# Hybrid Hyena and neighbourhood-attention step: activations and three weight blocks of a row block loaded in one transfer, with the order of the opening changed

## The chip, the cores and the metric

The kernel runs on one core of a Trainium2 chip. The metric is the device time of one execution in microseconds (us); a kernel's time is the median of its runs. Before the change it is 869.93 us, the median of three runs (867.72 to 872.84).

The engines are named as the profile names them: PE (TensorE, matrix products), PEld (its weight loads), DVE (VectorE), ACT (ScalarE), POOL (GpSimd) and SP (SyncE, which here only issues transfers).

## The reference

One layer of a network is applied to 128 context tokens and 512 latent tokens. Both groups share the weights. What matters here is the beginning: a modulation (scale, shift and gate) is computed from a condition, the tokens are scaled and shifted by it, and the result is projected by a wide matrix. The first three of the projected parts go through a short convolution; the filters of the long convolution come from a small network on a fixed embedding.

```python
shift, scale, gate = modulation(cond, p["w_ada"], p["b_ada"])   # silu(cond) @ w_ada + b_ada
h = x * (1 + scale) + shift
z = h @ w_in                       # (640, 1024) @ (1024, 10240), split into hy, g_h, qkv, g_a, m
hy = short_conv(hy, conv_w, conv_b)
hf = sin(f_freq[0] * (z_emb @ f_w1 + f_b1))      # the filter network, on a fixed embedding z_emb
hf = sin(f_freq[1] * (hf @ f_w2 + f_b2))
hf = (hf @ f_w3) * decay
...
x_new = layer_norm(ALPHA * x + gate * out, p["ln_g"], p["ln_b"])
```

## The kernel before, in words

The 640 tokens stand as columns; the 1024 channels are eight **row blocks** of 128. `hH` and `hL` hold the modulated tokens `h`, split into a high part (rounded to the type fp32r) and the rest, of the same type. The wide matrix is cut into column blocks of 128 columns, each a 128 x 1024 array in `a["wall"]`, eight 128 x 128 tiles side by side (one for each row block). A weight block is split in the same way, into `wh` and `wl`. A product of a row block with a column block is three passes, `wh` with `hH`, `wl` with `hH`, `wh` with `hL` (line 170, `accumulate`), each of two matmuls of 320 tokens: six matmuls, summed over the eight row blocks in two PSUM banks.

**The prologue** (lines 258 to 388) makes `h` one row block k at a time, and multiplies it at once with three column blocks, 0, 8 and 1, whose sums stay open over all eight k (`mm` for blocks 0 and 8, `mm1lo` and `mm1hi` for block 1). For each k it does this:

- Two transfers of 512 KB bring row block k's two parts of the modulation matrix (`ada`, line 247); PE multiplies them with the condition (`adaT`, line 253, 32 matmuls), ACT copies the result (`row`, line 328), and PE turns it (`modT`, line 357). DVE adds the bias (`mod`, line 362).
- A transfer brings the tokens of row block k (`xt`, from `xT`, 320 KB). DVE computes `hx` (line 369), ACT computes `hH` from the same operands (line 370, two instructions), and DVE takes the difference `hL` (line 378).
- The tiles of weight blocks 0, 8 and 1 come in four steps, not in eight: `SPAN` on line 277 gives columns 0 to 128 with k = 0, 128 to 256 with k = 1, 256 to 512 with k = 2 and 512 to 1024 with k = 3, so twelve transfers (`raw`, `w1r`). ACT makes the high parts (line 300), DVE and, for blocks 8 and 1 from k = 2 on, POOL the low parts (line 304).
- The table `script` says which products PE does at which of four places of an iteration: "00" is block 0 with row block 0, "81" is block 8 with row block 1, "w5" is five matmuls on a zeroed tile (line 270) that keep PE busy and whose result is not used.
- The filter network (`sin_layer`, from line 214, its products `ps_f` on line 221, its sines on line 234) advances by some steps in each iteration, as the table `layers` says.

Inside the prologue the order on PE, DVE and ACT is that of the code. SP issues its transfers in an order of its own queue; a transfer into a buffer that is still read waits, and everything behind it on SP waits too. `ada` has three buffers, `raw` three. The scheduler orders what stands behind the prologue.

Behind the prologue PE multiplies column block 9 (its split is the tile `w9`), then block 2, then 10, with the first filter spectrum between them. From block 2 on the low part of a weight block is not computed by DVE: ACT writes the negative of the raw block rounded (line 149), and a transfer issued by POOL adds the weights themselves onto it (line 150). The filter spectrum needs constants: a Fourier matrix (`draw`, from `dft`, split into `dftH` and `dftL`), a second small one (`gs`), the filter weights (`w3s`, `w3h`, `w3l`) and the convolution's weights (`pack2`).

## Time and profile before

| what | value |
|---|---|
| median of three runs | 869.93 us (867.72 to 872.84) |
| the profiled execution's own time | 871.15 us |
| its span, first to last instruction | 869.3 us |
| so outside the span | 1.85 us |
| PE busy | 856.0 us, 98% |
| DVE, ACT, POOL busy | 678.7, 465.5, 137.8 us |
| bytes moved | 139.17 MB, mean 160 GB/s |
| granted PE clock, mean of the span | 0.995 |

A row of the timeline gives the start in us from the span's start, the duration, the engine, the line, the operation, the output and input tiles with their shapes and, after x, how many instructions are merged in it; square brackets give the engine's idle time before it and what ended it. A row of the windows view gives for a stretch of time its length, then the busy time of PE, PEld, DVE, ACT and POOL (with counts), the granted PE clock as a share of full speed, the busy share of the transfer engines and the bytes per second that they moved.

### The profile page before, as it was taken

The numbers are of one execution on the slowest core, as the hardware profiler recorded it, in microseconds if no ns is written. First come the engines' busy times: TensorE is split into PE (matmuls) and PEld (weight loads), VectorE is DVE, ScalarE is ACT, GpSimd is POOL, SyncE is SP. The second block draws the span as 40 slices with busy tenths as digits, with TensorE's granted clock in tenths as the row PEclk, the third lists the DMA queues.
The fourth block names the chain that finished last, engine by engine and source line by source line (L and its number), as shares of the span: only waits on it lengthen the run. The fifth ranks groups of instructions, "written<-read, shape, count | busy, mean of one in ns | idle before, by whom it ended". The sixth has DMA issues, their size and how long they took to land.

```text
span 869.3 us, 16872 instructions
## 1 busy us (share of the span) xinstructions
PE 856.0 (98%) x6394; PEld 827.1 (95%) x6394; DVE 678.7 (78%) x1407; ACT 465.5 (54%) x1001; POOL 137.8 (16%) x146
## 2 busy tenths in 40 slices
PE   8899999999999999999999999999999999999996
PEld 7799999999999999999999999999999999999885
DVE  5476678669567865999987898889888769799776
ACT  4385554654645454547566566556666655345300
POOL 0210101010100101105222224024322200000000
PEclk9999999999999999999999999999999999999998
DMA  9987757456665647874343526263454376445621
GB/s 313 369 212 174 149 106 155 112 149 136 137 152 118 144 114 186 209 202 163 116 162 111 185 76 221 73 207 101 149 155 133 104 260 212 165 132 147 245 99 49
DMA packets 58740, 139.17 MB, mean 160 GB/s; under 512 B 8703, under 2 KB 25219, under 8 KB 58660
## 3 DMA queue, kind: packets, MB, share of 16 engines
q1 hardware_dynamic: 47140, 111.69, 39.0%
q0 software_dynamic: 5904, 20.71, 14.9%
q10 hardware_dynamic: 5616, 5.70, 1.9%
q8 instruction: 50, 0.82, 0.4%
q14 instruction: 30, 0.25, 0.1%
HBM read 121.96 MB, written 16.12 MB: 159 GB/s over the span
## 4 chain that ended last, share of the span: by engine, by line
PE 96%; DMA 3%; DVE 1%; ACT 0%; POOL 0%; issue 0%; DVEq 0%; POOLq 0%
PE sp L1195 33%; PE mm L170 31%; PE out L1548 6%; PE v L926 5%; PE pt L1028 3%; PE s L1035 3%; PE s L988 2%; PE mm L184 2%; DMA ada<-wada 2%; PE ve L938 1%; DMA wl<-wall 1%; PE adaT L253 1%; PE adaT L270 1%; PE yb L159 1%; PE yb L158 1%; PE yb L160 1%
## 5 line engine op out<-in xcount | busy, mean ns | idle before, releaser
L1195 PE MATMUL sp<-t,wb 128*128 128x320 f32 x912 | 142.0, 310 | 0.0
L1195 PEld LDWEIGHTS sp<-t,wb 128*128 128x128 f32 x912 | 135.2, 188 | 0.9 <-ACT pp L1056 0.5
L170 PE MATMUL mm<-hH,wh 128*128 128x320 f32 x480 | 113.3, 313 | 0.3 <-ACT hH L370 0.3
L170 PE MATMUL mm<-hL,wh 128*128 128x320 f32 x480 | 113.1, 311 | 0.0
L170 PE MATMUL mm<-hH,wl 128*128 128x320 f32 x480 | 112.9, 311 | 0.1
L1195 PE MATMUL sp<-hH,wb 128*128 128x320 f32 x456 | 111.2, 314 | 0.0
L170 PEld LDWEIGHTS mm<-hH,wh 128*128 128x128 f32 x480 | 80.2, 189 | 2.4 <-issue 1.2
L170 PEld LDWEIGHTS mm<-hH,wl 128*128 128x128 f32 x480 | 81.1, 189 | 1.1 <-DMA wl<-wall 0.5
L170 PEld LDWEIGHTS mm<-hL,wh 128*128 128x128 f32 x480 | 81.0, 189 | 0.9 <-DVE hL L378 0.4
L101 ACT ACTIVATE wb<-s 128x512 fp32r<-128x512 f32 x92 | 56.5, 629 | 45.9 <-DVE s L1155 26.7
L150 POOL DMA_DIRECT2D wl<-wall x38 | 33.1, 871 | 300.9 <-ACT wl L149 224.3
L1195 PEld LDWEIGHTS sp<-hH,wb 128*128 128x128 f32 x456 | 78.5, 188 | 2.3 <-issue 2.1
L151 ACT ACTIVATE wh<-raw 128x1024 fp32r<-128x1024 f32 x38 | 40.4, 1062 | 73.5 <-PE mm L170 65.4
L1195 PE MATMUL sp<-hL,wb 128*128 128x320 f32 x228 | 70.4, 309 | 0.0
L102 DVE TENSOR_TENSOR wb<-s,wb 128x512 fp32r<-128x512 f32 x92 | 62.5, 691 | 8.0 <-ACT wb L101 8.0
L101 ACT ACTIVATE wb<-raw 128x512 fp32r<-128x512 f32 x66 | 41.5, 628 | 47.3 <-PE sp L1195 23.4
L1010 POOL TENSOR_SCALAR p<-p,sm 128x384 f32<-128x384 f32 x32 | 44.6, 1406 | 101.7 <-DVE sm L1009 101.7
L102 DVE TENSOR_TENSOR wb<-raw,wb 128x512 fp32r<-128x512 f32 x66 | 46.5, 704 | 5.1 <-ACT wb L101 4.8
L170 PE MATMUL mm<-yhs,wh 128*128 128x320 f32 x256 | 47.9, 309 | 0.0
L1210 DVE TENSOR_TENSOR c<-sp,u 128x320 f32<-128x320 f32 x69 | 33.5, 486 | 12.1 <-PE sp L1195 12.1
L1195 PEld LDWEIGHTS sp<-hL,wb 128*128 128x128 f32 x228 | 42.9, 188 | 0.0
L1010 POOL TENSOR_SCALAR edge<-edge,sm 128x320 f32<-128x320 f32 x32 | 42.2, 1330 | 0.5 <-DVE sm L1009 0.5
(384 smaller groups left out, 2054.0 us busy)
## 6 DMA issues: line engine op xcount, KB each, us to landing
raw<-wall SPq DMA_DIRECT2D x93, 512.0 KB, 3.6
wl<-wall POOLq DMA_DIRECT2D x38, 512.0 KB, 5.8
ada<-wada SPq DMA_DIRECT2D x16, 512.0 KB, 7.0
tm<-bias SPq DMA_DIRECT2D x16, 512.0 KB, 4.9
gate<-wgate SPq DMA_DIRECT2D x8, 512.0 KB, 4.0
wo<-wall SPq DMA_DIRECT2D x8, 512.0 KB, 5.4
xt<-xT SPq DMA_DIRECT2D x8, 320.0 KB, 7.6
dec<-decay SPq DMA_DIRECT2D x20, 128.0 KB, 3.3
```

The source lines that it names most:

```text
L101: hi = nc.scalar.activation(dst_h, src, AF.Copy)
L102: return hi, (eng or nc.vector).tensor_tensor(dst_l, src, f(dst_h), op=ALU.subtract)
L150: nc.gpsimd.dma_start(wl, a["wall"][i], accum_op=ALU.add)
L151: nc.scalar.activation(wh, raw[:], AF.Copy)
L170: nc.tensor.matmul(ps[hf][:, :HALF], wt[k], x[:, hf * HALF : (hf + 1) * HALF], start=(i == 0 and k == 0), stop=(i == lead[2] and k == NK - ...
L926: nc.tensor.matmul(ps[t // 2][:, t % 2 * 256 : t % 2 * 256 + 256], x[:, k, P * t : P * t + P], wk, start=first and t % 2 == 0, stop=last, ...
L1010: nc.gpsimd.tensor_scalar_mul(pv, pv, sm[:, 2:3])
L1028: nc.tensor.transpose(pt[:, i * P : i * P + P], x, ident)
L1035: nc.tensor.matmul(dst, lhs, rhs, start=start, stop=stop, skip_group_check=True)
L1195: nc.tensor.matmul(dst, wk, x(xi, k), start=j < 4 and k == 0 and i == 0, stop=k == 3 and i == 2, skip_group_check=True,)
L1210: after = nc.vector.tensor_tensor(c, dst, c if j == 3 else u, op=ALU.add)
L1548: ins = nc.tensor.matmul(dst, m[k][:, c0 : c0 + P], w[:, c : c + n], start=(first and k == 0), stop=(last and k == 5), skip_group_check=True,)
```

## The change

The host lays out a new array `xw`: for each row block k the 640 tokens and, beside them, the three 128 x 128 tiles of weight blocks 0, 8 and 1 that belong to k. One transfer of 512 KB for each k brings both. `SPAN`, its twelve transfers and the functions around it are gone. ACT makes the three high parts of k in one instruction (`wf`, 128 x 384) and DVE the three low parts in one (`wg`); POOL has none of it. The tiles `xw` take the three buffers of `raw`.

The embedding and the first filter constants (`zemb`, 82.5 KB, and `pack1`, 98 KB) are loaded ahead of the modulation matrix, and the first filter layer starts among PE's opening matmuls. The product "00" moves from k = 0 to k = 1. `gs`, `skip`, `pack2` and the Fourier matrix are loaded behind the last row block, and the split of the Fourier matrix and of `gs` stands behind the prologue (`dft_high`, `dft_consts`, with `behind` setting who follows whom). Weight block 2 is split by ACT and DVE, without the adding transfer.

```diff
         script = (
-            ("w16", "w5", "w3", "w6 00"), ("", "", "80", "10"), ("", "", "01", "81 11"), ("", "", "02", "82 12"),
+            ("w8", "w3", "w8", ""), ("", "", "00", "80 10"), ("", "", "01", "81 11"), ("", "", "02", "82 12"),
...
-        layers = ((0, 4), (0, 2), (0, 1), (0, 1), (0, 1), (0, 3), (0, 3), (0, 1))
+        layers = ((0, 2), (1, 0), (1, 2), (0, 2), (0, 2), (1, 1), (0, 0), (0, 0))
...
-        SPAN = {0: (0, 128), 1: (128, 256), 2: (256, 512), 3: (512, 1024)}
...
-        def w_load(i, g):
-            load_to(span(i, g)[0], a["wall"][i][:, slice(*SPAN[g])])
...
+        out["zemb"] = temp("u", "zemb", 4)[:33]
+        load_to(out["zemb"], a["zemb"])
+        load_pack(1)
...
         for k in range(NK):
+            xw = wp.tile([P, 1024], F32, tag="raw", bufs=3, name=f"xw{k}")
             psa = aux(f"adaT{k}")
+            if k == 0:
+                work("w8", psa)
+                step(5)
...
+            load_to(xw[:], a["xw"][k])
+            xt, wf = xw[:, :NT], xw[:, NT:]
+            wh = row(yhp, "yh", f"wf{k}", F32R)[:, : 3 * P]
+            wl = row(yhp, "yh", f"wg{k}", F32R)[:, : 3 * P]
...
-            xt = row(yhp, "yh", f"xt{k}")
-            load_to(xt[:], a["xT"][:, k])
-            if k in SPAN:
-                for i in (8, 1) if k == 0 else (0, 8, 1):
-                    w_load(i, k)
...
+            if k >= 6:
+                split(wh, wl, wf)
+            if k == 7:
+                wraw(9)
                 load_pack(2)
...
+                wraw(2)
+                load_filter(0)
...
+                nc.scalar.activation(w9[:, 0], raws[9][:], AF.Copy)
...
-            if k == 3:
-                w_high(0, 3)
-            else:
-                for i in (8, 1) if k < 5 else ():
-                    w_high(i, min(k, 3))
-            if k in SPAN:
-                w_low(0, k)
+            if k < 6:
+                nc.scalar.activation(wh, wf, AF.Copy)
             nc.vector.tensor_tensor(hL[:, k], hx[:], f(hH[:, k]), op=ALU.subtract)
+            if k < 6:
+                nc.vector.tensor_tensor(wl, wf, f(wh), op=ALU.subtract)
...
-                early[2] = wtile(2, "dma")
+                early[2] = wtile(2)
...
         prologue()
-    tc.keep_in_program_order(last[0])
-    head = quarter_head(0)
-    next(head)
+        opening = list(last)
+        head = quarter_head(0)
+        next(head)
+        dft_high(0, 1)
+    tc.keep_in_program_order(opening[0])
     dft_consts()
```

How the order of the engines' instructions moves, at three places. The names are those of the program; a number behind a name is that of its buffer, and x with a count stands for equal instructions in a row.

**SP, from the program's first transfer to the second row block's.** Before:

```order
L63 DMA pack_80<-pack 128x34
L63 DMA ada_127<-wada 128x1024 x2
L63 DMA raw_169<-wall 128x128
L63 DMA xt_182<-xT 128x640
L63 DMA raw_172<-wall 128x128
L63 DMA w1r_175<-wall 128x128
L63 DMA pack_187<-pack 128x196
L63 DMA zemb<-zemb 33x640
L63 DMA ada_239<-wada 128x1024 x2
L63 DMA E<-gs 128x256
L63 DMA skip_719<-hydr 1x256
L63 DMA xt_260<-xT 128x640
```

And in the changed kernel (`pack_119` holds the first filter constants, `pack_187` above):

```order
L63 DMA pack_80<-pack 128x34
L63 DMA zemb<-zemb 33x640
L63 DMA pack_119<-pack 128x196
L63 DMA ada_157<-wada 128x1024 x2
L63 DMA xw_136<-xw 128x1024
L63 DMA ada_217<-wada 128x1024 x2
L63 DMA xw_215<-xw 128x1024
L63 DMA ada_275<-wada 128x1024 x2
L63 DMA xw_273<-xw 128x1024
```

Two small transfers now stand ahead of the first modulation matrix; behind it there are three transfers of 512 KB for each row block and nothing else.

**PE, from its first instruction to the second row block's modulation.** Before:

```order
L270 MATMUL adaT_126<-hid 128x256 x16
L253 MATMUL adaT_126<-ada_127,st 32x128 x8
L270 MATMUL adaT_126<-hid 128x256 x5
L253 MATMUL adaT_126<-ada_127,st 32x128 x8
L270 MATMUL modT_191<-hid 128x256 x3
L357 MATMUL modT_191<-pack_80,row_167 128x2 x2
L270 MATMUL modT_191<-hid 128x256 x6
L170 MATMUL mm_0_210<-hH,wh_170 128x320
```

In the changed kernel:

```order
L274 MATMUL adaT_137<-hid 128x256 x8
L225 MATMUL ps_f_147<-zemb,pack_119 64x320
L225 MATMUL ps_f_148<-zemb,pack_119 64x320
L274 MATMUL adaT_137<-hid 128x256 x8
L257 MATMUL adaT_137<-ada_157,st 32x128 x8
L274 MATMUL adaT_137<-hid 128x256 x3
L257 MATMUL adaT_137<-ada_157,st 32x128 x8
L274 MATMUL modT_192<-hid 128x256 x8
L339 MATMUL modT_192<-pack_80,row_187 128x2 x2
L257 MATMUL adaT_216<-ada_217,st 32x128 x16
L174 MATMUL mm_0_130<-hH,wf_190 128x320
L174 MATMUL mm_1_131<-hH,wf_190 128x320
```

The filter layer's products `ps_f` come among the filler matmuls, and the first product (`mm_0` from `hH`) stands behind the second row block's `adaT`, no longer ahead of it.

**ACT, from the last `hH` of the prologue to the first rounding for an adding transfer (`wl`, from `raw`).** Before:

```order
L370 ACTIVATE hH<-xt_617,mod_636 128x512
L101 ACTIVATE w_644<-raw_621 128x1024
L149 ACTIVATE wl_648<-raw_623 128x1024
L561 ACTIVATE zs_102<-mm_0_210 128x128
L563 ACTIVATE zs_102<-mm_0_210 128x8x8
L564 ACTIVATE zs_102<-mm_0_210 128x8x16
L151 ACTIVATE wh_647<-raw_623 128x1024
L234 ACTIVATE E<-E 128x640
```

In the changed kernel:

```order
L352 ACTIVATE hH<-xw_573,mod_627 128x512
L105 ACTIVATE wh_636<-raw_605 128x1024
L540 ACTIVATE zs_102<-mm_0_130 128x128
L542 ACTIVATE zs_102<-mm_0_130 128x8x8
L543 ACTIVATE zs_102<-mm_0_130 128x8x16
L544 ACTIVATE zs_102<-mm_1_131 128x8x40
L540 ACTIVATE zs_106<-mm_0_132 128x128
L542 ACTIVATE zs_106<-mm_0_132 128x8x8
L546 ACTIVATE u_670<-zs_102,pack_603 128x641
L380 ACTIVATE dftH<-draw 128x640 x2
```

The high part of block 9 (`w_644`), the rounding of block 2 (`wl_648`) and the second sine (`E` from `E`) no longer stand behind the last `hH`; the first two pieces of the Fourier matrix (`dftH`) now do.

More of the change, by code (lines that the diff above doesn't have):

```diff
@@ L259, in prologue, with warm @@
         script = (
-            ("w16", "w5", "w3", "w6 00"), ("", "", "80", "10"), ("", "", "01", "81 11"), ("", "", "02", "82 12"),
+            ("w8", "w3", "w8", ""), ("", "", "00", "80 10"), ("", "", "01", "81 11"), ("", "", "02", "82 12"),
             ("", "", "03", "83 13"), ("", "", "04", "84 14"), ("", "", "05", "85 15"), ("", "", "06", "86 16 07 87 17"),
         )
-        layers = ((0, 4), (0, 2), (0, 1), (0, 1), (0, 1), (0, 3), (0, 3), (0, 1))
+        layers = ((0, 2), (1, 0), (1, 2), (0, 2), (0, 2), (1, 1), (0, 0), (0, 0))
         nc.gpsimd.memset(f(hid[:, :256]), 0.0)
+        front = (0, 8, 1)
+        parts = {}
+        def warm(ps, n):
+            for _ in range(n):
+                nc.tensor.matmul(ps[:, 256:], hid[:, :P], hid[:, :256], start=True, stop=True, skip_group_check=True)
         def work(items, ps):
@@ L392, in prologue @@
         now(filt)
+        last.append(low)
     dftH = hyc.tile([P, 2, 5, 2, P], F32R, tag="dftH", name="dftH")
@@ L418, in dft_consts @@
         load_to(gs, two(a["gs"]))
+        behind(last[0], opening[0])
         split(gsH[:], gsL[:], gs)
@@ L442, in filter_spectrum @@
         load_to(skip[:], a["hydr"][q : q + 1])
+        if q == 0:
+            behind(last[0], opening[0])
         w3h = hwa.tile([P, 512], F32R, tag="w3h", name=f"w3h_{q}")
```

79 lines of the change are left out of this document (22 added, 57 removed).

## The prediction

> **What bounds the kernel now.** I read the page's first and fourth parts, then the windows view by stages, then the timeline of PE.
>
> ```profile
> span 869.3 us, 16872 instructions
> PE 856.0 (98%) x6394; PEld 827.1 (95%) x6394; DVE 678.7 (78%) x1407; ACT 465.5 (54%) x1001; POOL 137.8 (16%) x146
> PE 96%; DMA 3%; DVE 1%; ACT 0%; POOL 0%; issue 0%; DVEq 0%; POOLq 0%
> PE adaT L253 <- DMA ada<-wada: 2.9, 3, 1.7
> ```
>
> PE is the bound almost everywhere; the one wait of PE that the waits view finds of any size is for `ada`, at the start. So what an edit to the prologue is worth is read from the prologue alone: by how much sooner PE gets through it.
>
> ```profile
> 5.35:10.80 5.45, 4.94 (x51) 3.73 (x50) 1.18 (x5) 1.82 (x5) 0.00 (x0) 1.00 1.03 352
> 10.80:26.90 16.10, 14.87 (x169) 12.16 (x171) 13.35 (x29) 8.23 (x20) 2.00 (x2) 1.00 1.00 362
> 26.90:36.10 9.20, 7.35 (x58) 5.88 (x58) 2.88 (x7) 2.63 (x5) 2.62 (x2) 0.81 1.03 414
> 36.10:51.70 15.60, 15.57 (x180) 14.42 (x181) 11.48 (x22) 8.94 (x17) 0.81 (x1) 1.00 0.78 273
> 51.70:66.50 14.80, 14.70 (x99) 14.26 (x98) 11.43 (x16) 12.11 (x26) 1.95 (x3) 1.00 0.87 199
> ```
>
> Up to 36.1 us the transfer engines are full (1.00 and over) and PE has gaps; from 36.1 on PE is full and they are not. Between 26.9 and 36.1 the granted PE clock is 0.81. So the prologue is bound by transfers, then by a slow clock, and by PE alone only in its last third. While small pieces (rows of 512 and 1024 bytes of `raw` and `w1r`) were among the transfers they moved 352 to 362 GB/s; later, with rows of 2 KB and more, 414.
>
> ```profile
> 26.88 0.64 PE L253 MATMUL adaT<-ada,st 128*32 128x128 f32 x16 [1.07 <-DMA ada<-wada]
> 29.24 0.64 PE L253 MATMUL adaT<-ada,st 128*32 128x128 f32 x16 [1.71 <-DMA ada<-wada]
> 31.16 0.87 PE L170 MATMUL mm<-hH,wh 128*128 128x320 f32 x2
> 34.62 1.34 PE L221 MATMUL ps_f<-hf,pack 64*128 64x320 f32 x4
> 40.43 1.08 PE L253 MATMUL adaT<-ada,st 128*32 128x128 f32 x32
> 42.79 0.54 PE L170 MATMUL mm<-hH,wh 128*128 128x320 f32 x2
> 44.73 1.08 PE L253 MATMUL adaT<-ada,st 128*32 128x128 f32 x32
> 51.60 0.31 PE L170 MATMUL mm1hi<-hL,w1h 128*128 128x320 f32 x1
> ```
>
> In the full part one row block takes PE 44.73 - 40.43 = **4.30 us** (1.0 for `adaT`, 0.36 for `modT`, 18 products at 0.147, the rest gaps; 0.147 is a twelfth of the stretch from 42.79 to 44.73 less its gap of 0.18). The rows at 26.88 and 29.24 are the two waits, and the pair at 31.16 takes 0.87 where the one at 42.79 takes 0.54: the slow clock. The last matmul of the prologue starts at 51.60; block 9's first follows at 51.74.
>
> **The change, part by part.** I count to two marks: t1, when PE has done row block 1's `modT`, and t7, the same for row block 7.
>
> ```profile
> 1.18 0.89 SPq L63 DMA_DIRECT2D ada<-wada  x2
> 1.64 3.78 PE L270 MATMUL adaT<-hid 128*128 128x256 f32 x16 [1.64 <-POOL spare L312]
> 5.35 1.08 PE L253 MATMUL adaT<-ada,st 128*32 128x128 f32 x16
> 6.37 1.27 PE L270 MATMUL adaT<-hid 128*128 128x256 f32 x5
> 7.57 0.65 PE L253 MATMUL adaT<-ada,st 128*32 128x128 f32 x16
> 9.58 0.96 PE L270 MATMUL modT<-hid 128*128 128x256 f32 x6 [0.25 <-DVE mod L362]
> 12.16 1.29 PE L221 MATMUL ps_f<-zemb,pack 33*64 33x320 f32 x4
> 15.37 0.50 PE L357 MATMUL modT<-pack,row 128*128 128x2 f32 x4
> 46.73 0.50 PE L357 MATMUL modT<-pack,row 128*128 128x2 f32 x4
> ```
>
> With the next PE instruction 0.36 us behind the start of `modT`, t1 is now 15.7 and t7 47.1, 31.4 apart; five full row blocks would be 21.5 of that.
>
> *The opening.* Up to about 7.6 us a filler takes 0.24 us (3.78 / 16), at 9.58 only 0.16. The early products run at the slow pace, and for `ps_f` no row shows that: its bounds are 1.29 as at 12.16 and twice that. I take 2.1, the ratio of the pairs at 31.16 and 42.79 (0.87 / 0.54 = 1.6) times 1.29. PE then does 8 fillers, `ps_f`, 8 fillers in 3.78 + 2.1 from 1.64: 7.5. Two `adaT` halves at 0.65, three fillers 0.5, eight fillers 1.25 and `modT` 0.55 bring row block 0's `modT` to 11.1. (`ada` arrives earlier: two more issues, at 0.89 / 2 each, on SP and 180 KB ahead of it put it about 1 us behind now, when PE took its first half at 5.35 without waiting for it.)
>
> *The first products, now behind `adaT` 1.* They need the chain `modT`, `mod`, `hH`, `hL`, `wg`:
>
> ```profile
> 20.98 0.42 DVE L304 TENSOR_TENSOR wl<-raw,wh 128x256 fp32r<-128x256 f32 x1
> 25.93 0.69 DVE L304 TENSOR_TENSOR wl<-raw,wh 128x512 fp32r<-128x512 f32 x1 [0.95 <-ACT wh L300]
> 42.97 0.16 DVE L362 TENSOR_TENSOR mod<-modT,bss 128x4 f32<-128x4 f32 x1 [0.24 <-PE modT L357]
> 43.16 1.21 ACT L370 ACTIVATE hH<-xt,mod 128x128 fp32r<-128x128 f32 x2 [1.14 <-DVE mod L362]
> 44.40 0.83 DVE L378 TENSOR_TENSOR hL<-hx,hH 128x640 fp32r<-128x640 f32 x1 [0.43 <-ACT hH L370]
> 45.14 1.68 DVE L230 SCALAR_TENSOR_TENSOR E<-E 128x640 f32<-128x640 f32 x2
> 46.85 0.49 DVE L232 TENSOR_SCALAR E<-E 128x640 f32<-128x640 f32 x1
> ```
>
> No row shows `wg`, 128x384; between 0.42 and 0.69 I take 0.55. From `mod`'s start: `hH` ends at 1.40, `hL` at 2.26, `wg` at 2.8. So from 11.1 the first row block's `wg` is there at 13.9, while PE has finished `adaT` 1 at 12.1 and waits (its first pass, 0.3, fits into that). Two more passes, 0.6, and `modT` 0.35: **t1 = 14.9**, 0.8 sooner than now.
>
> *Row blocks 1 to 7.* PE needs 4.30 for each, and 1.2 more in the second, where the second filter layer's products now stand. 6 x 4.30 + 1.2 = 27.0, against 31.4: 4.4 saved, the two waits and the slow clock. What covers the rest:
> - `wg`, at `mod` + 2.8, is asked for at `mod` + 3.3 (12 products 1.77, gap 0.2, `adaT` 1.0, the first pass 0.3). Cover 0.5.
> - DVE has per row block the chain to 2.8 and at most two filter steps, 1.68 less overlaps: 4.4. That may lose 0.1 once; it takes 0.55 for `wg` in place of its own low parts now, and POOL's, of which there are none left.
> - ACT, busy for 8.94 of 15.60 us in the full part, gets `wf` (128x384) in place of the three high parts.
> - Transfers: 1.57 MB per row block, 3.8 us at 414 GB/s and 4.3 at 362. From a bulk start at about 3 us even the slower rate brings `ada` 7 (12.3 MB) to 37, some 2 us ahead of its use at t7 - 2.5. SP's queue holds three kinds of waits, for `ada`'s readers, for DVE's `wg` three row blocks before, and for an earlier transfer; each of them is answered at least two row blocks ahead.
>
> t7 = 14.9 + 27.0 = **41.9**, now 47.1.
>
> *The last products and behind.* From t7: 12 products of blocks 8 and 1 at k = 6, then 18 at k = 7, 30 x 0.147 = 4.4, and about 0.2 of waiting for `hL`, as ACT now makes `w9`'s high part (below, 1.04) ahead of the last `hH`. 46.5 in place of 51.7: **5.2 saved**. Behind it block 2 no longer waits for an adding transfer:
>
> ```profile
> 48.57 1.04 ACT L101 ACTIVATE w<-raw 128x1024 fp32r<-128x1024 f32 x1
> 60.10 0.30 PEld L170 LDWEIGHTS mm<-hH,wl 128*128 128x128 f32 x2 [0.54 <-DMA wl<-wall]
> 58.28 1.14 ACT L149 ACTIVATE wl<-raw 128x1024 fp32r<-128x1024 f32 x1
> 59.72 0.87 POOL L150 DMA_DIRECT2D wl<-wall x1 [7.80 <-ACT wl L149]
> DMA to landing us min/median/max: 5.6/7.2/9.2
> ```
>
> PE's own rows lose only 0.1 there (14.80 less 14.70), so I credit 0.1. Late next is block 10, whose `wl` starts on ACT now at 58.28. Between the last `hH` and it ACT loses `w9`, block 2's rounding, a sine and `hid`, and gains `dftH` and `gs`, about 1.8 us fewer; the last `hH` ends at t7 + 1.7. That puts it at 51.4, POOL's issue at 52.8, landing by 5.6 to 9.2 at 58.4 to 62.0. PE asks for it after blocks 9 and 2 (96 products, 14.1), two filter products (about 0.5) and four of its own (0.6): at 61.7. I take 0; its bounds are 0 and 0.3 as worked out, up to 2 when ACT is held up.
>
> *Far behind,* the scheduler put some instructions of the attention stage in another order, of the same kinds and number. No row prices that. PE's idle time after 66.5 is 7.9 us in all:
>
> ```profile
> 66.50:869.30 802.80, 794.89 (x5829) 773.11 (x5827) 637.86 (x1328) 428.78 (x926) 129.30 (x123) 1.00 0.53 149
> ```
>
> I take 0, with 1 us either way.
>
> **Sum**: -0.8 - 4.4 - 0.1 = **-5.3**. The profiled execution took 871.15 (its span of 869.3 and 1.85 around it), 1.22 over the median of the runs; it would take 865.9, and the median **864.6**.
>
> **The rivals.**
> - *The slow clock comes back.* It followed a stretch in which PE did 0.64 us of work in 3.4 (25.8 to 29.2), and cost 3.46 us for 12 products (31.16 to 34.62) that take 1.77 otherwise. In the changed opening PE idles for about 1.4 of 3.4 us ahead of the first `wg`. If that is enough, the next 12 products and `adaT` cost some 2.3 more: 866.9. Against it: the gaps are shorter and PE has done 9 us of work. [...]
> - *Block 10's low part is late.* ACT and POOL run later by up to 2 us: 866.6. For it: 9.2 is the longest landing in just this stretch. Against it: ACT has less to do.
> - *The change doesn't do what it says:* transfers bind on, at 362 GB/s, and t1 slips as `ada` 1 comes at 12.5. A rate of 362 costs nothing by the sum above, so only t1 slips, to 15.5, with 0.5 of waits later: 865.7.
> - *Slower.* The three `xw` buffers close a loop: transfer k + 3 is issued when DVE has done `wg` of k, 2.8 us behind its `mod`, and must have landed at `mod` k + 3. A round is then (2.8 + landing) / 3. At the longest landing of now, 10.3 of `ada` under full queues, that is 4.37, no matter. To eat up the 5.3 over the five rounds that reuse a buffer, each must take 5.36: landings over 13.3 us; to lose 0.5%, 4.35 us more, over 15.9. Then 870 to 875.
>
> ```profile
> DMA to landing us min/median/max: 4.5/7.0/10.3
> ```
>
> **How the numbers follow.** Forecast 0.60 (its own range 862.8 to 866.4: t1 moves by 0.8 with the bounds of `ps_f` and of the filler pace, the attention stage by 1). Clock 0.12, block 10 0.11, transfers 0.09, slower 0.08. The range for eight in ten takes in all but the slower case and the ends of the clock's and of block 10's: **862.0 to 868.4**. A difference of 0.5%, about what a measurement of this kernel can tell from no change, is 4.35 us, so faster begins at 865.6. Some three quarters of the forecast's range lie below it, and half of the transfers' case; with a little off for the spread of the runs, faster 0.55. Slower than 874.3 needs the loop near its worst: 0.05. The rest, 0.40, is within 0.5%.
>
> **What would show it.** No wait of PE for `ada` past the second row block; the clock at 1.00 from 12 us on; `adaT` every 4.3 us; t1 near 14.9 and t7 near 41.9; block 9's first product at 46.5 rather than 51.7; no idle PE at block 10's `wl`. Wrong would be: `adaT` starts more than 4.5 apart with a releaser in DVE (`wg`) or in the transfers, a clock under 1 between 12 and 20 us, or a start of block 9 near 46.5 and a span that has not followed it.

## The result, and the profile after

The changed kernel takes **867.63 us** (median of 22 runs, 866.34 to 869.46); the kernel before, run beside it, 869.34 (22 runs, 867.72 to 872.84). The ratio is 0.9982 [0.9974, 0.9991]: 1.7 us sooner by the medians, 0.2%. The forecast was 864.6 and a gain of more than 0.5%. The time lies inside the range, but the gain is a third of what was forecast. The profiled execution took 866.75, with a span of 865.0.

The page of the changed kernel, the engines' busy time and the shares of the chain that ended last:

```profile
PE 854.4 (99%) x6391; PEld 825.5 (95%) x6391; DVE 680.8 (79%) x1408; ACT 464.6 (54%) x996; POOL 132.1 (15%) x141
PE 99%; DVE 1%; ACT 0%; POOL 0%; issue 0%; DVEq 0%; POOLq 0%
```

and PE's waits in the prologue, from the waits view (total, times, longest):

```profile
PE mm L174 <- ACT wf L354: 0.9, 1, 0.9
PE mm L174 <- DVE wg L357: 0.4, 1, 0.4
```

The 3% of the chain that belonged to transfers is gone, and so are all waits for `ada`. What is left is two waits at the first products, where the prediction had put them. The windows view of the changed kernel, by stages (the granted PE clock is the third figure from the right):

```profile
5.35:10.80 5.45, 5.45 (x45) 3.69 (x43) 3.52 (x6) 0.00 (x0) 0.00 (x0) 1.00 1.01 401
...
26.90:36.10 9.20, 9.20 (x114) 8.41 (x113) 7.89 (x16) 5.07 (x11) 0.00 (x0) 1.00 0.95 350
36.10:48.20 12.10, 12.10 (x132) 11.11 (x131) 9.07 (x18) 9.08 (x20) 0.00 (x0) 1.00 0.75 257
```

From 26.9 to 48.2 PE is full and its clock is 1.00. In the first row PE is busy all of the time too, but it gets through 45 matmuls where the kernel before did 51. The two kernels' matmuls there are not the same ones, so the count alone proves nothing; PE's timeline shows their durations:

```profile
1.64 2.08 PE L274 MATMUL adaT<-hid 128*128 128x256 f32 x8 [1.64 <-POOL spare L294]
3.73 2.36 PE L225 MATMUL ps_f<-zemb,pack 33*64 33x320 f32 x4
6.02 2.07 PE L274 MATMUL adaT<-hid 128*128 128x256 f32 x8
8.03 1.08 PE L257 MATMUL adaT<-ada,st 128*32 128x128 f32 x16
10.98 1.22 PE L274 MATMUL modT<-hid 128*128 128x256 f32 x8
12.03 0.50 PE L339 MATMUL modT<-pack,row 128*128 128x2 f32 x4
...
14.43 0.56 PE L174 MATMUL mm<-hH,wf 128*128 128x320 f32 x2 [0.89 <-ACT wf L354]
15.35 0.56 PE L174 MATMUL mm<-hH,wg 128*128 128x320 f32 x2 [0.35 <-DVE wg L357]
43.15 0.50 PE L339 MATMUL modT<-pack,row 128*128 128x2 f32 x4
48.20 0.31 PE L174 MATMUL mm<-hH,w 128*128 128x320 f32 x1
```

Eight fillers take 2.07 (0.26 each) at 6.02, and a half of `adaT` 1.08 at 8.03, where 0.65 is full pace. Only the eight fillers at 10.98 are fast (1.22). PE works at a slow pace for the first 11 us, while the granted clock reads 1.00. So t1 is 16.41 (`modT` 1 starts at 16.04, the next PE instruction 0.37 later; 14.9 was forecast, 15.7 was before), t7 is 43.51 (41.9 forecast), and block 9 starts at 48.20 (46.5 forecast, 51.74 before). Behind it the kernel takes 865.0 - 48.2 = 816.8, before 869.3 - 51.74 = 817.6: between these two traces nothing is given back later.

### The profile page after: what moved, and what is told of

Its sections match the earlier page's. It is cut to its first block, busy times and chain, and to the rows that moved or that the text cites. A ratio compares the mean times of both kernels' runs of the same rounds, so it can differ in the third digit from the quotient of the medians.

```text
span 865.0 us, 16825 instructions
## 1 busy us (share of the span) xinstructions
PE 854.4 (99%) x6391; PEld 825.5 (95%) x6391; DVE 680.8 (79%) x1408; ACT 464.6 (54%) x996; POOL 132.1 (15%) x141
## 4 chain that ended last, share of the span: by engine, by line
PE 99%; DVE 1%; ACT 0%; POOL 0%; issue 0%; DVEq 0%; POOLq 0%
PE sp L1172 33%; PE mm L174 32%; PE out L1525 6%; PE v L907 5%; PE pt L1009 3%; PE s L1016 3%; PE s L969 2%; PE mm L188 2%; PE ve L919 1%; PE adaT L257 1%; PE adaT L274 1%; PE yb L163 1%; PE yb L162 1%; PE yb L164 1%; PE ut L601 1%; PE fl L436 1%
## 5 line engine op out<-in xcount | busy, mean ns | idle before, releaser
L174 PE MATMUL mm<-hH,wh 128*128 128x320 f32 x448 | 105.1, 311 | 0.0
L174 PE MATMUL mm<-hL,wh 128*128 128x320 f32 x448 | 105.0, 310 | 0.0
L174 PE MATMUL mm<-hH,wl 128*128 128x320 f32 x448 | 104.3, 310 | 0.0
L174 PEld LDWEIGHTS mm<-hH,wh 128*128 128x128 f32 x448 | 75.3, 188 | 0.7
L174 PEld LDWEIGHTS mm<-hH,wl 128*128 128x128 f32 x448 | 75.4, 188 | 0.5
L174 PEld LDWEIGHTS mm<-hL,wh 128*128 128x128 f32 x448 | 75.5, 188 | 0.4
L106 DVE TENSOR_TENSOR wb<-raw,wb 128x512 fp32r<-128x512 f32 x66 | 46.5, 704 | 5.8 <-ACT wb L105 5.6
```

The source lines that it names most:

```text
L106: return hi, (eng or nc.vector).tensor_tensor(dst_l, src, f(dst_h), op=ALU.subtract)
L174: nc.tensor.matmul(ps[hf][:, :HALF], wt[k], x[:, hf * HALF : (hf + 1) * HALF], start=(i == 0 and k == 0), stop=(i == lead[2] and k == NK - ...
```

## The experiments

**The kernels again, for their traces.** Theory A: the profiled execution of before had a stretch of slow clock that is not in every execution, and in the changed kernel PE is slow for longer at the start. Theory B: the prologue's gain is given back later.

*e1, the kernel before, unchanged.*

> The kernel before, unchanged, profiled a second time. Theory A (the profiled execution of before was a slow one for itself: its PE clock fell at 31 to 36 us, worth about 2.3 us, and most executions are spared that): block 9's first product starts near 49.5 us instead of 51.74, the granted clock between 27 and 36 us is 0.95 or more, span near 867. Theory B (the prologue gains over 3.5 us in every execution, and later stages give half of it back): the prologue ends at 51.5 to 52 again, and the span less the prologue's end is some 2 us shorter than in the changed kernel.

870.63 us, span 868.8. *e2, the same again.*

> The same once more, for the spread between executions. Theory A: the end of the prologue and the granted clock up to 36 us move together from execution to execution, by 1 to 3 us, and the rest of the span stays within 0.5 us. Theory B: the prologue's end is the same within 0.5 us.

868.97 us, span 867.1. The stretch in which the prediction had seen a clock of 0.81, in e1 and then in e2, by the windows view:

```profile
26.90:36.10 9.20, 7.46 (x67) 5.76 (x70) 3.58 (x8) 2.68 (x6) 1.51 (x2) 0.81 1.03 414
```

```profile
26.90:36.10 9.20, 7.90 (x99) 6.38 (x98) 4.37 (x8) 3.74 (x8) 2.62 (x2) 1.00 1.03 413
```

e1 has the slow clock, e2 has not, and does 99 matmuls where e1 does 67. PE's timeline in e2, `modT` 1, `modT` 7 and block 9's first product:

```profile
15.38 0.50 PE L357 MATMUL modT<-pack,row 128*128 128x2 f32 x4
44.67 0.50 PE L357 MATMUL modT<-pack,row 128*128 128x2 f32 x4
49.68 0.31 PE L170 MATMUL mm<-hH,w 128*128 128x320 f32 x1
```

and its waits for `ada`:

```profile
PE adaT L253 <- DMA ada<-wada: 2.4, 3, 1.2
```

The same kernel with nearly the same waits (2.4; 2.9 in the first trace) reaches block 9 at 49.68 instead of 51.74. From t1 to t7 it needs 29.3, not 31.4: 0.5 of the difference is the shorter waits, the rest goes to the clock. In e1 the waits for `ada` come to 3.8, one of them 2.0 right ahead of the slow products (PE's timeline); in the first trace it was 1.7, in e2 the longest is 1.2. So in the two slow traces a longer wait and the slow clock come together:

```profile
28.26 0.98 PE L253 MATMUL adaT<-ada,st 128*32 128x128 f32 x16 [2.02 <-DMA ada<-wada]
```

From block 9 to the end it is 817.4 in e2 and 817.3 in e1. Theory A holds, and B falls. How often: beside the experiments the kernel before ran 98 times; in 62 of these executions the mean granted clock was 0.997 or more, with a median span of 866.9; in 36 it was 0.996 or less, with a median span of 869.45. So the executions with the lower mean clock are about 2.5 us longer, and they are over a third. Only three of the kernel's executions were traced: the first one and e1, with the stretch, have mean clocks of 0.995 and 0.996, and e2, without it, has 0.998. That the others at 0.996 or less have the same stretch is inferred from their mean clock.

*e3 and e11, the changed kernel, unchanged.*

> The changed kernel, unchanged, profiled again. Theory A: the rounds stay at 4.30 us, the filler pace is slow up to some point between 7 and 12 us, the prologue ends at 46.5 to 49 accordingly; from there to the end 816 to 817.5 us as in before. Theory B: from the prologue's end to the last instruction at least 819.

> The changed kernel, unchanged, once more for its trace: the two traces of it so far took 865.0 and 864.5, while its executions range to 867.7 with granted clocks down to 0.995. If this one is a long execution (over 866.5): Theory A' (a spell of slow clock also comes in the changed kernel) shows a stretch of the prologue or right behind it with a clock under 0.9 and matmuls at more than 0.2 us; the rival (block 10's low part comes late at times) shows a wait of PE for `wl` of 0.5 to 2. If it is a short one it shows neither: block 9 at 47.8 to 48.3.

e3: 866.31, span 864.5, block 9 at 47.80; from the third row block on `adaT` stands 4.30 apart, as in the first trace. e11: 867.35, span 865.6, block 9 at 47.83. Neither has the slow clock; e11's 1.1 more is behind the prologue, 0.6 of it a wait for an adding transfer far behind it, of which e3 has none.

*e15, the changed kernel a fourth time.*

> The changed kernel once more for its trace. If it is a long execution: a slow stretch (matmuls of `mm` over 0.2 us between 12 and 60 us, or the fast pace later than 11 us), or waits for adding transfers (`wl`, `wb`; the third trace had one of 0.6) that make up the difference to 864.5. If it is a short one: block 9 at 47.8 to 48.3 and no such wait.

868.40, span 866.6: this is a long one, and the slow clock is in it. The windows view of e15:

```profile
14.00:16.60 2.60, 2.14 (x13) 1.88 (x14) 2.48 (x6) 0.68 (x3) 0.00 (x0) 1.00 1.03 418
16.60:20.50 3.90, 3.90 (x43) 3.34 (x41) 1.95 (x4) 1.88 (x4) 0.00 (x0) 0.56 1.01 389
```

and PE's timeline, the first products, block 9's first and block 10's first low part:

```profile
14.10 0.56 PE L174 MATMUL mm<-hH,wf 128*128 128x320 f32 x2 [0.89 <-ACT wf L354]
15.02 0.56 PE L174 MATMUL mm<-hH,wg 128*128 128x320 f32 x2 [0.36 <-DVE wg L357]
16.76 0.73 PE L174 MATMUL mm<-hL,wf 128*128 128x320 f32 x2
49.41 0.31 PE L174 MATMUL mm<-hH,w 128*128 128x320 f32 x1
65.09 0.56 PE L174 MATMUL mm<-hH,wl 128*128 128x320 f32 x2 [0.40 <-DMA wl<-wall]
```

Right behind the two waits, 1.25 us in all, the clock is 0.56 for 3.9 us, and a pair of products takes 0.73 instead of 0.46. The same two waits stand in the other three traces of this kernel, and there the clock stays at 1.00: the waits come ahead of the slow clock, but it does not follow them every time. Block 9 starts 1.6 later than in e11. Both of the prediction's small rivals are in this execution: the slow clock (1.6; 2.3 was said) and block 10's low part (0.4). The 22 runs of the changed kernel have 6 with a clock of 0.996 or less (median span 867.1; the other sixteen 865.65).

**e4: does idle PE bring the slow clock?** The kernel before, with 22 fillers ahead of `ada` of row block 4:

```diff
-            ("", "", "03", "83 13"), ("", "", "04", "84 14"), ("", "", "05", "85 15"), ("", "", "06", "86 16 07 87 17"),
+            ("w8", "w14", "03", "83 13"), ("", "", "04", "84 14"), ("", "", "05", "85 15"), ("", "", "06", "86 16 07 87 17"),
```

> The kernel before with 8 and 14 filler matmuls in front of the two halves of row block 4's modulation product, where PE waited 1.07 and 1.71 us. Theory A: PE no longer idles there, the clock stays at 1.00 up to 36 us, block 9 starts at 49 to 50 us in the profile; in time 0 to 2 us faster than before, by how often the slow clock visits it. Theory B: nothing moves but the clock, 0 to 0.3 us.

869.67, ratio 1.0012 [1.0002, 1.0022]. None of its 11 executions has a clock of 0.996 or less, and in 26.9 to 36.1 its trace shows PE busy for 9.03 us at 1.00:

```profile
26.90:36.10 9.20, 9.03 (x98) 7.64 (x96) 2.94 (x6) 3.01 (x6) 2.63 (x2) 1.00 1.05 413
```

That agrees with the theory but does not settle it: of the 15 executions of the unchanged kernel beside these only 3 have the lower clock, so none in 11 can be chance. The time is not gained: block 9 starts at 49.32 in the trace, near e2's 49.68, and the median span of 867.9 is 1.0 over the 866.9 of the kernel before at 0.997 or more. PE starts the second half of `adaT` 4 at 28.34 there and at 28.70 in e2, 0.36 apart, as block 9 is.

**e5 and e8, e16: is PE's way through the opening what sets the time?** First with eight fillers less:

```diff
-            ("w8", "w3", "w8", ""), ("", "", "00", "80 10"), ("", "", "01", "81 11"), ("", "", "02", "82 12"),
+            ("", "w3", "w8", ""), ("", "", "00", "80 10"), ("", "", "01", "81 11"), ("", "", "02", "82 12"),
```

> The changed kernel without the second eight filler products (those behind `ps_f`, 2.07 us at 6.02 in its trace). Theory A (in the opening PE itself is late: it works through fillers at 0.26 us while row block 0's `ada` has landed): PE takes `ada` 0 at about 6.2 instead of 8.0, every later mark moves by 1.5 to 2.0, the median goes from 867.6 to 865.6 to 866.1. Rival (the fillers only fill a wait for transfers, or without them the slow pace lasts the longer): the first products keep their place at 14.4 and the median stays within 0.4 of 867.6.

865.75, ratio 0.9965 [0.995, 0.998]. As expected by the median, but the traced execution is one of the longer (866.0; the eight spans go from 863.3 to 866.5). In it PE waited 1.1 for the constants and was slow well into `adaT` 1, which takes 1.51 where 1.08 is full pace (the waits view, one line, and PE's timeline):

```profile
PE ps_f L225 <- DMA pack<-pack: 1.1, 1, 1.1
```

```profile
10.08 2.08 PE L274 MATMUL modT<-hid 128*128 128x256 f32 x8
12.73 1.51 PE L257 MATMUL adaT<-ada,st 128*32 128x128 f32 x32
```

Block 9 starts at 48.47 there, no sooner than in the changed kernel. So no trace shows where the shorter executions gain, and Theory A rests on the median alone.

Then with row block 0's weights split ahead of `mod`:

```diff
-            if k >= 6:
+            if k in (0, 6, 7):
                 split(wh, wl, wf)
...
-            if k < 6:
+            if 0 < k < 6:
```

> The changed kernel with the high and low part of row block 0's three weight blocks made ahead of its `mod` instead of behind its `hH` and `hL` (as it does at row blocks 6 and 7). In the trace of the changed kernel PE waits 0.89 for `wf` and 0.35 for `wg` there, and ACT and DVE were idle for 3 to 7 us ahead of `mod`. Theory A (t1 is late by work on the path): the wait for `wf` becomes one of 0.4 for `hH`, `wg`'s goes, 0.8 is saved and stays saved to the end: median 866.6 to 867.0. Rival (the transfers of row block 1 or 2 bind right behind): the waits move to `ada` or to `mod` of row block 1 and the median stays within 0.3 of 867.6.

> The early split alone, a second time (e8: 865.82 over 6 runs, 1.8 under the changed kernel, where its trace showed 0.8 to 0.9). Theory A: 0.8 is the edit's, median 866.4 to 867.0. Rival (the edit also removes waits in the opening that in some executions bring a slow clock): median 865.5 to 866.2 again and no execution with a granted clock under 0.997.

e8: 865.82, ratio 0.9956 [0.9942, 0.997]. e16, the same kernel: 866.11, ratio 0.9964 [0.995, 0.9977]. In e8's trace PE waits once (the waits view), and block 9 starts at 47.45, 0.75 sooner than in the changed kernel's first trace and 0.4 sooner than in e3 and e11:

```profile
PE mm L174 <- ACT hH L352: 0.5, 1, 0.5
```

e16's block 9 starts at 47.36, but its trace then waits 1.45 for block 10's low part (span 865.9). Both times the median falls by more than the traces show (1.5 to 1.8). All twelve executions have a clock of 0.997 or more, against 16 of 22: with the two waits down to one of 0.5, none has e15's mean clock of 0.996. That may be a part of the rest; but among the executions at 0.997 or more the median spans still differ by 1.3 to 1.6 (864.05 and 864.35 against 865.65), and why by more than the trace's 0.75 stays open. This version beats the kernel before in both measurements; e8's interval lies under the changed kernel's, e16's overlaps it a little. With eight fillers less the kernel before is beaten as well, the changed one by the medians alone.

**e9: both edits together.**

> The changed kernel with both edits: row block 0's weights split ahead of `mod`, and no second eight fillers behind `ps_f`. Theory A (both stand on PE's path in the opening, one behind the other): their savings add, 0.8 of waits and 1.5 to 2.0 of fillers, block 9 starts at 45.5 to 46.2, median 863.8 to 865.0. Rival (block 10's low part, whose adding transfer PE waited 1.3 for in the run with the embedding later, where block 9 started at 47.21, is a floor near): block 9 starts as early, but PE waits 1 to 2 for `wl`, median 865.3 to 866.0, no better than either edit alone.

867.13, ratio 0.9964 [0.995, 0.9979], no better than either alone. The rival's reason, block 10's low part, is 0.62 us in its trace, less than the 1 to 2 that it named; the opening shows another. The twelve spans go from 863.4 to 866.7, all at a clock of 0.997 or more. PE's timeline in the traced one, 865.6:

```profile
6.46 1.08 PE L257 MATMUL adaT<-ada,st 128*32 128x128 f32 x16 [0.37 <-DMA ada<-wada]
12.08 1.93 PE L257 MATMUL adaT<-ada,st 128*32 128x128 f32 x32
13.94 0.90 PE L174 MATMUL mm<-hH,wf 128*128 128x320 f32 x2
```

PE starts `adaT` 0 at 6.46 instead of 8.03 and has lost it again by block 9 (47.91): `adaT` 1 takes 1.93 instead of 1.08, and the first pairs of products take 0.90, 0.73 and 0.73 up to 15.7, where e8's take 0.56, 0.46 and 0.56. How long the slow pace lasts is not fixed: in the two traces with fewer fillers it lasted into `adaT` 1 (e5, 1.51) and to 15.7 (e9), in the changed kernel's to 10 or 11.

**e6: the embedding and `ps_f` later.**

```diff
-        out["zemb"] = temp("u", "zemb", 4)[:33]
-        load_to(out["zemb"], a["zemb"])
-        load_pack(1)
...
             load_to(xw[:], a["xw"][k])
+            if k == 0:
+                load_pack(1)
+                out["zemb"] = temp("u", "zemb", 4)[:33]
+                load_to(out["zemb"], a["zemb"])
+                filt = hidden_layers()
```

The filter network's steps (`layers`) are those of the kernel before as well.

> The changed kernel with the embedding and its constants loaded behind row block 0's activations and the first filter layer's products `ps_f` run later, as before the change; the rest of the change stays. Theory A (what the change moved to the front of PE's and SP's queue costs what it takes at the slow pace, 2.4 us for `ps_f` and 0.85 us of issue): `modT` 0 starts at 8.5 to 9.5 instead of 12.0, `ps_f` costs 1.3 later, block 9 starts 1.5 to 2.3 sooner, median 865.3 to 866.3. Rival (the opening's order is not on the path; the slow pace ends by a time or by an amount of work that this edit does not change): median 867.0 to 868.0.

867.76, ratio 0.9984 [0.9972, 0.9995]: the same as the changed kernel. The opening did what Theory A said (PE's timeline, to block 10):

```profile
8.55 0.50 PE L340 MATMUL modT<-pack,row 128*128 128x2 f32 x4
8.98 1.29 PE L225 MATMUL ps_f<-zemb,pack 33*64 33x320 f32 x4
47.21 0.31 PE L174 MATMUL mm<-hH,w 128*128 128x320 f32 x1
63.75 0.56 PE L174 MATMUL mm<-hH,wl 128*128 128x320 f32 x2 [1.25 <-DMA wl<-wall]
```

`modT` 0 starts at 8.55 instead of 12.03 and `ps_f` takes 1.29 instead of 2.36, yet block 9 starts only 1.0 sooner: `ps_f` now stands behind it, and waits for `hH`, `wf` and `wg` take 1.7. Then 1.25 of it goes to block 10's low part, and four of the twelve executions have a clock of 0.996 or less (median span 867.3; the other eight 865.85). So for the time it does not matter whether the embedding and the filter layers stand as before or as in the change.

**e7: four transfers in place of one.**

```diff
-            load_to(xw[:], a["xw"][k])
+            load_to(xw[:, :NT], a["xw"][k][:, :NT])
+            for c in range(NT, 1024, P):
+                load_to(xw[:, c : c + P], a["xw"][k][:, c : c + P])
```

> The changed kernel with each row block's activations (rows of 1280 bytes) and its three weight blocks (rows of 512 bytes each) loaded by four transfers in place of one: the loading of before in this one respect. If the small rows cost what the prediction said (362 in place of 414 GB/s, 4.3 us per row block against PE's 4.30), PE waits for `ada` or `wf` by 0.5 to 1.5 in all: median 868.1 to 869.1, and that is the part of the change that brings its gain. If transfers have slack at either rate: median within 0.3 of 867.6, DMA at 360 GB/s in the opening and no new wait.

867.40, ratio 0.9975 [0.9964, 0.9986]: nothing lost. There is no wait for `ada` in its trace, at 377 GB/s from 16.0 to 26.9. Merging the transfers brings nothing by itself that the time shows.

**e10: the kernel before, with its weights in eight pieces.**

```diff
-        SPAN = {0: (0, 128), 1: (128, 256), 2: (256, 512), 3: (512, 1024)}
+        SPAN = {g: (P * g, P * g + P) for g in range(NK)}
...
-            if k == 3:
-                w_high(0, 3)
-            else:
-                for i in (8, 1) if k < 5 else ():
-                    w_high(i, min(k, 3))
+            for i in (8, 1):
+                w_high(i, k)
...
-            for i in (8, 1) if k in (0, 1, 2, 4) else ():
-                w_low(i, min(k, 3))
+            for i in (8, 1):
+                w_low(i, k)
```

All low parts are on VectorE, and block 0's high parts are made in every row block.

> The kernel before with the three early weight blocks loaded, rounded and subtracted in eight pieces of 128 columns, one per row block, instead of four pieces that have brought all 1024 columns by row block 3; nothing else of the change. Theory C (before, PE waited for `ada` 2, 3 and 4 because 0.75 MB of weights that are used only from row block 4 on went ahead of them; the change's gain in the rounds is that these go later): the waits of 2.4 to 2.9 for `ada` go, block 9 starts at 48.0 to 48.7 instead of 49.7 to 51.7, no execution has a granted clock of 0.996 or less, median 866.6 to 867.6. Rival (the gain is from the first products standing one row block later, which gives PE's queue work to do): the waits for `ada` stay above 1.5 in all and the median stays within 0.4 of 868.7, or is above it as ACT and DVE have more pieces to do.

872.57, ratio 1.0032 [1.0016, 1.0048]: slower. The waits for `ada` come to 1.2 in all (2.4 to 3.8 in the three traces of the unchanged kernel), and others take their place (the waits view):

```profile
PE mm L170 <- ACT hH L369: 1.6, 2, 1.3
PE adaT L253 <- DMA ada<-wada: 1.2, 2, 0.7
PE mm L170 <- ACT zs L560: 0.6, 1, 0.6
```

Theory C fails as stated: this edit does not give the gain. It is no clean test of the weights' order, though, as it also gives ACT and DVE more pieces: PE waits 1.6 for `hH`, which ACT makes, where the kernel before waits 0.3.

**e12: block 2's low part by an adding transfer, as before.**

```diff
-                early[2] = wtile(2)
+                early[2] = wtile(2, "dma")
```

> The changed kernel with block 2's low part made as before, by ScalarE's negated rounding and an adding transfer issued on GpSimd, instead of a subtraction on VectorE. The prediction credited 0.1 for this part; from block 9's first product to the end the traces of the changed kernel take 0.6 to 0.9 less than those of before. If this part brought that: the stretch is 817.4 again and the median 868.2 to 868.6. If not: the median stays within 0.3 of 867.6.

868.19, ratio 0.9982 [0.9968, 0.9997]. The ratio is that of the changed kernel, so the time does not tell them apart. The trace does: block 9 starts at 47.81, as in e11, and PE then waits for block 10, from block 9 to the end 818.5:

```profile
64.47 0.56 PE L174 MATMUL mm<-hH,wl 128*128 128x320 f32 x2 [1.20 <-DMA wl<-wall]
```

In the four traces of the changed kernel that wait is 0, 0, 0 and 0.4, and from block 9 to the end they take 816.8, 816.7, 817.8 and 817.2, where three traces of the kernel before take 817.6, 817.3 and 817.4. So the changed kernel's gain behind block 9 is not sure to be more than these differences between executions, and one trace of e12 does not show that block 2's split brings it.

**e13, e17 and e14, e18: what ends the slow pace?** Theory D: full products without a break. The instructions of the changed kernel, with sixteen fillers in a row ahead of `ps_f`:

```diff
-            ("w8", "w3", "w8", ""), ("", "", "00", "80 10"), ("", "", "01", "81 11"), ("", "", "02", "82 12"),
+            ("", "w3", "w8", ""), ("", "", "00", "80 10"), ("", "", "01", "81 11"), ("", "", "02", "82 12"),
...
-                work("w8", psa)
+                work("w16", psa)
                 step(5)
```

> The changed kernel with its first sixteen filler products in one row ahead of the first filter layer's products `ps_f`, instead of eight ahead and eight behind: the same instructions in another order, loads as in the change. Theory D (the slow pace ends after some 4 to 5 us of products that use the whole array; `ps_f`, 33 x 64, does not count): the fast pace comes at 5.5 to 7.5 us instead of 10 to 11, `ps_f` takes 1.3 to 2.1, row block 0's `modT` starts at 9.5 to 10.5 instead of 11.7 to 12.0, block 9 at 46.0 to 46.8 instead of 47.8 to 48.2; median 865.8 to 866.8, unless block 10's low part takes up to 1 of it. Rival (the slow pace ends at a time of its own, or with an amount of work): `modT` 0 at 11.5 to 12.1 as in the change, median within 0.4 of 867.5.

> e13's kernel a second time. Theory D: most executions have spans of 862.0 to 862.7, some 865 to 867; the median is 863.8 to 864.6 again. If the traced one is short: the fast pace (fillers at 0.16 or less, the halves of `adaT` at 0.65) from 5.4 to 8 us on, `modT` 0 at 9.3 to 10.3, block 9 at 45.2 to 45.9, no slow stretch in 16 to 20. Rival (the short executions gain elsewhere): a short trace has block 9 at 47 or later and less time behind it than 816.5.

e13: 864.13, ratio 0.9938 [0.9926, 0.9951]. e17, the same kernel on another chip: 867.61 over twelve executions, ratio 0.9962 [0.9947, 0.9977]. One of the twelve took 1567.49 at a mean clock of 0.834, for a cause that is not known; the ratio leaves it out, and without it the median is 867.35. e13 has six spans of 862.1 to 862.6 and one of 866.5; e17's other eleven go from 863.3 to 866.4, without any such group, so its expectation of 863.8 to 864.6 failed. With the early split added:

> The sixteen fillers in a row, and row block 0's weights split ahead of `mod`. Theory D with both savings on the path: block 9 at 45.2 to 46.1, median 864.8 to 866.0, with a wait of PE for block 10's `wl` of 0.5 to 2 as the next bound. Rival: no more than the early split alone (e8).

> e14's kernel a second time, for its trace. Short (span 862.0 to 862.6): fast pace from 5.4 to 8 us on and block 9 at 44.5 to 45.5, with a wait for block 10's `wl` of 0.3 to 1.5 that eats the early split's 0.8. Long (865 to 866): the slow pace to 14 us or later.

e14: 864.38, ratio 0.9952 [0.9935, 0.9969]; four spans of 862.0 to 862.6 and three of 865.2 to 865.7. e18: 864.51, span 862.7. The traces show both kinds. PE's timeline in e13, a long one (866.5):

```profile
5.35 2.39 PE L225 MATMUL ps_f<-zemb,pack 33*64 33x320 f32 x4
16.18 0.90 PE L174 MATMUL mm<-hH,wg 128*128 128x320 f32 x2
49.39 0.31 PE L174 MATMUL mm<-hH,w 128*128 128x320 f32 x1
```

and in e18, a short one (862.7):

```profile
5.36 1.30 PE L225 MATMUL ps_f<-zemb,pack 33*64 33x320 f32 x4
12.27 0.46 PE L174 MATMUL mm<-hH,wg 128*128 128x320 f32 x2
45.29 0.31 PE L174 MATMUL mm<-hH,w 128*128 128x320 f32 x1
```

Up to 5.36 us the two go the same way (the sixteen fillers take 3.78 and 3.79), and then one runs at the slow pace (`ps_f` 2.39, a pair of products 0.90) to 17 us and the other at the fast one (1.30, 0.46) from there on. Block 9 starts 4.1 us apart, and the spans end 3.8 apart. These two kernels also differ by the early split. e14's trace is of e18's own kernel, and slow (PE's timeline, span 865.6):

```profile
5.35 2.39 PE L225 MATMUL ps_f<-zemb,pack 33*64 33x320 f32 x4
13.29 1.52 PE L257 MATMUL adaT<-ada,st 128*32 128x128 f32 x32
48.27 0.31 PE L174 MATMUL mm<-hH,w 128*128 128x320 f32 x1
```

Its slow pace lasts into `adaT` 1, and against e18 block 9 starts 3.0 later and the span is 2.9 longer. So the pace in the opening is worth more than the whole change (2.9 of span against 1.7 of the median), and the executions of one kernel differ by it. e17's trace (865.6) shows a third way: fast from 5.25, then two waits for `ada` 1 (PE's timeline), and the clock falls (the windows view):

```profile
10.58 0.64 PE L257 MATMUL adaT<-ada,st 128*32 128x128 f32 x16 [0.86 <-DMA ada<-wada]
11.77 1.03 PE L257 MATMUL adaT<-ada,st 128*32 128x128 f32 x16 [0.54 <-DMA ada<-wada]
```

```profile
12.70:18.60 5.90, 5.90 (x26) 5.62 (x22) 3.33 (x7) 2.73 (x5) 0.00 (x0) 0.50 1.03 416
```

In this trace PE is early, outruns the transfers, idles for 1.4 us and runs at a clock of 0.50 up to 18.6. Theory D is half right: that the pace decides is shown; that sixteen full products in a row bring it is not, as e13's and e14's traces had them and stayed slow. What decides between the two kinds stays open.

## Why the prediction was wrong, step by step

- **The step that failed is the base of the sum.** "It would take 865.9, and the median 864.6" took off the profiled execution's 1.22 over the median as if the changed kernel's execution would have the same excess; and "4.4 saved, the two waits and the slow clock" booked the slow clock as saved. Both are the same microseconds: the slow clock was why that execution was long. e2 without it needs 29.3 for the rounds, not 31.4, so from an undisturbed execution the term of 4.4 is 2.2. In numbers: the profiled execution of before lay 1.81 over the final median, that of after 0.88 under its own, so -4.40 between the two traces (871.15 to 866.75) is -1.71 between the medians. Of the miss of 3.0, 1.2 is the excess taken off twice; 0.9 is that the changed kernel's traced execution was one of its shorter ones, which no term of the sum provided for; and 0.9 is that this execution took 866.75 where 865.9 was forecast.
- **The opening was mis-sized.** "Up to about 7.6 us a filler takes 0.24 us" took the end of the slow pace from the trace of before; in the changed kernel it ended at 10 to 11, and t1 came at 16.4, not 14.9. So this term, forecast as 0.8 saved, was 0.7 lost. `ps_f` at 2.36 lay over the 2.1 chosen but under the upper bound, twice 1.29, which no trace reached (the longest is 2.39, in e13 and e14); `wg` at 0.55 was right. The 1.5 by which t1 came late, less what the traced execution gained behind block 9, is the last 0.9 of the miss.
- **The time of row blocks 1 to 7 was right, what it was compared with was not**: 27.1 for 27.0, `adaT` every 4.30 from the third on, no wait for `ada` nor for the `xw` ring. The clock of 1.00 from 12 us on held through the prologue in three traces of four.
- **The last products and behind**: 4.69 for 4.6. Behind block 9 the gain is 0.8 between the first two traces, where 0.1 was credited; over all seven traces of the two kernels it lies between a loss of 0.5 and a gain of 0.9, so the 0.1 is not refuted.
- **The rivals.** The slow clock comes back: it does, in some executions (e15, 1.6 us; 6 of the 22 have a mean clock of 0.996 or less). That the time lies inside the range does not show the sum right. Gaps shorter than the 1.07 and 1.71 of before and 9 us of work were the arguments against it, and they did not keep it off: in e15's trace 0.89 and 0.36 of idle time within 2 us went ahead of a clock of 0.56, and in e17 0.86 and 0.54 ahead of one of 0.50. The same waits as in e15 were followed by 1.00 in three other traces, so idle time of this size is not shown to be enough alone. The slow start varies as well: in e13 and e17, one kernel, the fast pace came at 17 us and at 5.3. Block 10's low part: 0.4 once in four traces, 0.26 to 1.45 in seven traces of the edited kernels and none in others (e8, e14, e17). Transfers bind and the slower ring: neither was seen in the changed kernel; the 377 GB/s of e7 cost nothing, and no run tried the 362 that the prediction allowed for.
- **What brought the gain** is less sure than that it is there. It is not the merged transfer (e7), nor the embedding ahead (e6), nor the order of the weights as e10 tried it. What is left is the first products one row block later, with the weights that this allows to come later; this was not tried by itself, and the cause stays open. Among executions at 0.997 or more the median spans are 866.9 before and 865.65 after, 1.25 apart, though not measured side by side; that fewer executions have the lower clock (6 of 22 against 36 of 98) may be the rest, but the counts are too small to show it.

## What to carry to other kernels

Before a saving is booked from a profiled execution, ask what makes this execution longer than the median, and do not take the same excess off twice: more traces of the unchanged kernel would have shown 2 us of the forecast's 5.3 to be the execution's own (one was not enough: e1 still had the slow clock, e2 had not). In an opening, PE's pace is to be read from the duration of its products, not from the granted clock (1.00 in the changed kernel both where eight fillers took 2.07 and where they took 1.22), and not to be carried over from another order of instructions (the slow pace ended at 7.6 us in the trace of before, at 10 to 11 in those of the changed kernel). Idle time of 1.25 us in e15 was followed by a slow clock that put block 9 1.6 later, and 1.40 in e17 by one at which 18 products and `modT` 1 (12.72 to 18.68) took 5.96, against 3.56 in e18; in three other traces of the changed kernel the same 1.25 was followed by a clock of 1.00. Work that fills it from what is there already (the early split) brought 1.5 and 1.8 by the medians, more than the 0.75 by which it cut the waits (1.25 to 0.5), by a cause that is only partly known.

## What the hardware showed that was not expected

- The granted clock reads 1.00 in the first 5 to 17 us of these traces while products run at a slow pace (in e13, at 1.00 in all rows of the windows view up to 66 us, the pair at 16.18 takes 0.90, 0.46 otherwise); later slow stretches do show in it (0.56 in e15, 0.50 in e17).
- The slow start of one and the same kernel ended at 5.3 us or at 17 us (e17, e13), with PE busy from 1.64 on, and in e13 the one long span lies 4 us over the other six.
- A mean granted clock of 0.996 or less went with spans 2.5 us longer in 36 of 98 executions of the kernel before; with the idle time filled (e4) it was in none of 11, and in 3 of the 15 of the kernel before beside them.
